# Short store runs beside long load runs, and Exp ahead of Ln, at the end of a streaming log-sum-exp scan

## Chip, cores, metric

One core of one Trainium2 chip. The metric is the device time of one execution in microseconds (us). A ratio is the mean time of one kernel's runs over that of the other's runs of the same rounds, so it is not quite the ratio of the medians quoted beside it. The span of a profile is about 1.7 us shorter than the time of the same run.

## The reference

For x of shape 8 x 4096 x 2048 (float32), a running log-sum-exp along the second axis:

```python
out[:, 0, :] = x[:, 0, :]
for t in range(1, S):
    mx = np.maximum(out[:, t-1, :], x[:, t, :])
    out[:, t, :] = mx + np.log(np.exp(out[:, t-1, :] - mx) + np.exp(x[:, t, :] - mx))
```

The kernel computes it as Ln of the prefix sum of Exp, 268 MB in and 268 MB out.

## The kernel before

A tile is 128 partitions x 4 rows x 2048 columns, 4 MiB; there are 64, numbered 0 to 63. A partition's four rows are neighbours in memory, so a whole tile moves as 128 runs of 32 KiB (a run is one contiguous piece, one record of data in the trace), 8 for each of 16 DMA engines (1213 ns a run in the trace). Four input buffers `ti`, two output buffers `to`. SP issues the loads, ACT issues the stores; the profile has one queue for each (q1 for loads, q10 for stores). A turn, below, is one record that an engine takes from one of its two queues. The semaphore write with which a DMA ends on an engine is a record of its own, of 4 bytes and 9 ns. The profile does not number the engines; what the text says of one engine was put together from the records, each of which begins where another ends, to 3 or 4 ns. While both queues hold work, the engines alternate between them: from 50 to 1110 us of this trace 15674 of 15767 records have one successor that no other record could have, and it is of the other queue every time, after the 1746 semaphore writes among them too.

```python
def exp(n, h, ...):                 # h: half of the columns
    if h == 0: take(act, loaded[n % NI], 16)
    act.activation(t[..half(h)], t[..half(h)], ACT.Exp).then_inc(exps[h], 1)

def ln(n, h, turn, in_place=False):
    if h == 0 and not in_place:
        take(act, stored[n % NO], 16)          # store of tile n-2 has left the buffer
    act.activation((ti if in_place else to)..., ti..., ACT.Ln)._wait_ge(carried[h], turn + 1)
# main loop, tiles 0..59
exp(n, 0); exp(n, 1); ln(n - 1, 0, ..); ln(n - 1, 1, ..)
event(act, [(logs, 2 * n)], [(freed, "sem-add-imm", 1)])   # lets SP load tile n + 3
act.dma_start(out=o_v[..][0], in_=to[(n - 1) % NO][:])
# ... the end, tiles 60..63, Ln in place in ti (no buffer wait):
for n in range(first + 1, NT):
    up = n - 1
    if n < NT - 1:
        exp(n, 0); exp(n, 1); ln(up, 0, .., True); ln(up, 1, .., True); store(up)
    else:                                      # n == 63
        ln(up, 0, .., True); exp(n, 0); ln(up, 1, .., True); store(up); exp(n, 1)
for h in range(2):
    ln(NT - 1, h, .., True); store(NT - 1, h)   # last store in two halves, runs of 4 KiB
```

DVE does six adds of row to row per tile, and two "joins" that add the carries from PE to all rows.

The softmax here doesn't subtract the row's maximum and nothing guards it: scores larger than these inputs give would overflow.

## Time and profile before

| | before |
|---|---|
| time, median of 4 runs | 1253.85 us (1253.28 to 1257.28) |
| span of the profile | 1252.5 us |
| DVE busy, ACT busy | 82%, 73% |
| moved | 537 MB at 429 GB/s |

The prediction below shows the slices and ACT's end. Here is the timeline of DVE from tile 60 on (start, duration, operation; in brackets how long DVE had stood idle before it, and for whom):

```profile
1161.74 7.40 DVE L248 TENSOR_TENSOR ti<-ti 128x1024 f32<-128x1024 f32 x6 [3.26 <-ACT ti L133]
1169.36 8.75 DVE L257 TENSOR_TENSOR ti<-ti,ps 128x4096 f32<-128x4096 f32 x2 [0.22 <-PE ps L224]
1181.60 7.40 DVE L248 TENSOR_TENSOR ti<-ti 128x1024 f32<-128x1024 f32 x6 [3.49 <-ACT ti L133]
...
1219.52 3.74 DVE L248 TENSOR_TENSOR ti<-ti 128x1024 f32<-128x1024 f32 x3 [5.58 <-ACT ti L133]
1227.06 3.75 DVE L248 TENSOR_TENSOR ti<-ti 128x1024 f32<-128x1024 f32 x3 [3.79 <-ACT ti L133]
```

A tile costs DVE 7.40 + 8.75 us. The waits in brackets are for Exp: DVE is not the bound of the kernel, but in the last tiles, where no more work overlaps, its holes count. The last two lines are tile 63: its first Exp half came behind an Ln half of tile 62, its second behind the other half.

### The profile page before, as it was taken

The numbers are of one execution on the slowest core, as the hardware profiler recorded it, in microseconds if no ns is written. First come the engines' busy times: TensorE is split into PE (matmuls) and PEld (weight loads), VectorE is DVE, ScalarE is ACT, GpSimd is POOL, SyncE is SP. The second block draws the span as 40 slices with busy tenths as digits, with TensorE's granted clock in tenths as the row PEclk, the third lists the DMA queues.
The fourth block names the chain that finished last, engine by engine and source line by source line (L and its number), as shares of the span: only waits on it lengthen the run. The fifth ranks groups of instructions, "written<-read, shape, count | busy, mean of one in ns | idle before, by whom it ended". The sixth has DMA issues, their size and how long they took to land. (4 is left out here: it accounts for less than half of the span.)

```text
span 1252.5 us, 3677 instructions
## 1 busy us (share of the span) xinstructions
PE 649.2 (52%) x960; PEld 214.1 (17%) x960; DVE 1023.0 (82%) x512; ACT 913.2 (73%) x258; POOL 1.1 (0%) x8
## 2 busy tenths in 40 slices
PE   2565356563664545546455553465545655346552
PEld 0121112121121211112112111121111111111110
DVE  5999788797887977878778788787887878878784
ACT  5886776777767668677686776867768668676884
POOL 0000000000000000000000000000000000000000
PEclk9988687876868868788687787877867777688785
DMA  9999999999999999999999999999999999999997
GB/s 402 419 435 434 429 433 431 433 433 435 435 434 430 432 431 433 434 434 435 434 430 432 431 433 434 434 435 434 429 434 430 433 434 435 434 434 429 435 430 303
DMA packets 19490, 536.90 MB, mean 429 GB/s; under 512 B 2080, under 2 KB 2080, under 8 KB 3104
## 3 DMA queue, kind: packets, MB, share of 16 engines
q1 hardware_dynamic: 9360, 268.44, 49.8%
q10 hardware_dynamic: 10128, 268.44, 49.7%
q8 instruction: 1, 0.02, 0.0%
q14 instruction: 1, 0.01, 0.0%
HBM read 268.44 MB, written 268.44 MB: 429 GB/s over the span
## 5 line engine op out<-in xcount | busy, mean ns | idle before, releaser
L248 DVE TENSOR_TENSOR ti<-ti 128x1024 f32<-128x1024 f32 x384 | 464.7, 1224 | 206.9 <-ACT ti L133 198.2
L140 ACT ACTIVATE to<-ti 128x4096 f32<-128x4096 f32 x120 | 427.6, 3609 | 248.4 <-ACTq L62 244.7
L257 DVE TENSOR_TENSOR ti<-ti,ps 128x4096 f32<-128x4096 f32 x128 | 560.0, 4417 | 9.5 <-PE ps L224 9.0
L224 PE MATMUL ps<-ti,before 128*128 128x512 f32 x512 | 381.2, 896 | 351.5 <-DVE ti L248 351.0
L133 ACT ACTIVATE ti<-ti 128x4096 f32<-128x4096 f32 (+1 forms) x128 | 452.6, 3582 | 59.9 <-ACTq L62 59.4
L213 PE MATMUL ps<-ti,last 128*128 128x512 f32 x448 | 268.2, 729 | 233.9 <-DVE ti L257 233.9
L224 PEld LDWEIGHTS ps<-ti,before 128*128 128x128 f32 x512 | 128.9, 279 | 617.9 <-DVE ti L248 510.8
L213 PEld LDWEIGHTS ps<-ti,last 128*128 128x128 f32 x448 | 85.3, 211 | 401.0 <-DVE ti L257 335.5
L140 ACT ACTIVATE ti<-ti 128x4096 f32<-128x4096 f32 x8 | 28.7, 3606 | 14.6 <-PEq L62 8.9
L153 ACT ACTIVATE ti<-ti 128x4096 f32<-128x4096 f32 x1 | 3.6, 3616 | 6.3 <-ACTq L62 6.3
L34 ACT ACT_TABLE_LOAD x1 | 1.3, 1283 | 0.8 <-PEq L286 0.8
L106 POOL TENSOR_SCALAR_AFFINE_SELECT last<-last 128x128 f32<-128x128 f32 x1 | 0.3, 295 | 0.0
L101 POOL TENSOR_SCALAR_AFFINE_SELECT before<-before 128x128 f32<-128x128 f32 x1 | 0.3, 294 | 0.1
L97 POOL MEMSET before<- 128x128 f32 x1 | 0.2, 205 | 0.5 <-SPq L80 0.5
L98 POOL MEMSET last<- 128x128 f32 x1 | 0.2, 205 | 0.0
L286 POOL MEMSET const-bfloat16-1.0<- 128x1 bf16 x1 | 0.1, 102 | 0.0
L286 POOL MEMSET const-uint8-127<- 128x1 uint8 x1 | 0.1, 102 | 0.0
L286 POOL MEMSET const-float32-0.0<- 128x1 f32 x1 | 0.1, 99 | 0.3 <-issue 0.3
L286 POOL MEMSET const-float32-1.0<- 128x1 f32 x1 | 0.1, 99 | 0.0
## 6 DMA issues: line engine op xcount, KB each, us to landing
ti<-in_x_dram SPq DMA_DIRECT2D x63, 4096.0 KB, 33.9
out_dram<-to ACTq DMA_DIRECT2D x60, 4096.0 KB, 31.4
out_dram<-ti ACTq DMA_DIRECT2D x3, 4096.0 KB, 22.4
ti<-in_x_dram SPq DMA_DIRECT2D x2, 2048.0 KB, 9.5
out_dram<-ti ACTq DMA_DIRECT2D x2, 2048.0 KB, 7.4
```

The costliest lines, as they stand in the source:

```text
L34: nc.scalar.preload_act_table_set("natural_log_exp_and_others")
L97: g.memset(before[:], 1.0).then_inc(ones, 1)
L101: g.affine_select(out=before[:], in_=before[:], compare_op=mybir.AluOpType.is_ge, fill=0.0, base=-1, pattern=[[1, P]], channel_multiplier= ...
L106: g.affine_select(out=last[:], in_=last[:], compare_op=mybir.AluOpType.is_ge, fill=0.0, base=-(P - 1), pattern=[[0, P]], channel_multiplier=1,
L133: act.activation(t[:, rows, half(h)], t[:, rows, half(h)], ACT.Exp).then_inc(exps[h], 1)
L140: act.activation((ti[n % NI] if in_place else to[n % NO])[:, :, half(h)], ti[n % NI][:, :, half(h)], ACT.Ln,)._wait_ge(carried[h], turn + ...
L153: act.activation(ti[0][:, 0:2, :], ti[0][:, 0:2, :], ACT.Exp)
L213: m = pe.matmul(ps[(k + 1) % 2][:, sl], last[:], ti[k % NI][:, R - 1, sl], start=True, stop=False, skip_group_check=True,)
L224: m = pe.matmul(ps[k % 2][:, sl], before[:], ti[k % NI][:, R - 1, sl], start=k == 0, stop=True, skip_group_check=True,)
L248: a = dve.tensor_add(t[:, r, half(h)], t[:, r - 1, half(h)], t[:, r, half(h)])
L257: dve.tensor_add(t[:, :, half(h)], t[:, :, half(h)], ps[n % 2][:, half(h)].unsqueeze(1).to_broadcast([P, R, HALF]),)._wait_ge(ahead[h], n ...
L286: nc = _bacc.Bacc("TRN2", target_bir_lowering=False, num_devices=1)
```

## The change

The intent: while the last loads are in flight, cut the stores into short runs, so that the DMA engines, which in the records alternate between the queues (all of those 15674 pairs), give the loads the larger part; and at the end do Exp of the next tile before Ln of the tile above, so that DVE gets its work early. The main loop ends four tiles sooner. The stores of tiles 56 to 59 become four DMAs of one row each (8 KiB runs); the last store becomes one again. The diff, cut to its core:

```diff
+                for n in range(first + 1, first + NI + 1):      # tiles 56..59
+                    up = n - 1
+                    exp(n, 0)
+                    exp(n, 1)
+                    ln(up, 0, up - first, stores_of=R if up >= first + NO else 1)
+                    ln(up, 1, up - first)
+                    event(act, [(logs, 2 * (n - first))], [(freed, "sem-add-imm", 1)])
+                    for r in range(R):
+                        act.dma_start(
+                            out=o_v[up][:, r, :], in_=to[up % NO][:, r, :]
+                        ).then_inc(stored[up % NO], 16)
... (cut)
-                    else:
-                        ln(up, 0, up - first, True)
-                        exp(n, 0)
-                        ln(up, 1, up - first, True)
-                        finals += store(up)
-                        exp(n, 1)
-                for h in range(2):
-                    ln(NT - 1, h, NT - 1 - first, True)
-                    finals += store(NT - 1, h)
+                    if n < NT:
+                        exp(n, 0)
+                        exp(n, 1)
+                    ln(up, 0, up - first, in_place=True)
+                    ln(up, 1, up - first, in_place=True)
+                    act.wait_ge(logs, 2 * (n - first))
+                    act.dma_start(out=o_v[up], in_=ti[up % NI][:]).then_inc(final, 16)
```

More of the change, by code (lines that the diff above doesn't have):

```diff
@@ L135, in exp, with ln @@
                     ).then_inc(exps[h], 1)
-                def ln(n, h, turn, in_place=False):
+                def ln(n, h, turn, in_place=False, stores_of=1):
                     if h == 0 and not in_place:
-                        take(act, stored[n % NO], 16)
+                        take(act, stored[n % NO], 16 * stores_of)
                     act.activation(
@@ L155, in _ @@
                 exp(0, 1, slice(2, R))
-                turns = (NT - 2) // NI
+                turns = (NT - 2) // NI - 1
                 with act.Fori(0, turns) as j:
@@ L171, in _ @@
                 first = turns * NI
-                finals = 0
-                def store(n, h=None):
-                    cols = slice(0, D) if h is None else half(h)
-                    act.wait_ge(logs, 2 * (n - first) + (2 if h is None else h + 1))
-                    act.dma_start(
-                        out=o_v[n][:, :, cols], in_=ti[n % NI][:, :, cols]
-                    ).then_inc(final, 16)
-                    return 1
-                for n in range(first + 1, NT):
-                    up = n - 1
-                    if n < NT - 1:
+                for n in range(first + 1, first + NI + 1):
+                    up = n - 1
+                    exp(n, 0)
[7 more added lines that the diff above has]
+                        ).then_inc(stored[up % NO], 16)
@@ L185, in _ @@
+                settle(NI)
+                first += NI
+                for n in range(first + 1, NT + 1):
+                    up = n - 1
+                    if n < NT:
                         exp(n, 0)
                         exp(n, 1)
-                        ln(up, 0, up - first, True)
-                        ln(up, 1, up - first, True)
-                        finals += store(up)
-                    else:
-                        ln(up, 0, up - first, True)
-                        exp(n, 0)
-                        ln(up, 1, up - first, True)
-                        finals += store(up)
-                        exp(n, 1)
@@ L196, in _ @@
-                for h in range(2):
-                    ln(NT - 1, h, NT - 1 - first, True)
-                    finals += store(NT - 1, h)
+                    ln(up, 0, up - first, in_place=True)
+                    ln(up, 1, up - first, in_place=True)
+                    act.wait_ge(logs, 2 * (n - first))
+                    act.dma_start(out=o_v[up], in_=ti[up % NI][:]).then_inc(final, 16)
                 settle(NT - first)
                 for n in range(NO):
-                    take(act, stored[n], 16)
@@ L202, in _ @@
-                take(act, final, 16 * finals)
+                    take(act, stored[n], 16 * R)
+                take(act, final, 16 * (NT - first))
             @block.tensor
```

## The prediction

Its sum: 1243.7 + 1.3 + 9.7 + 1.8 = 1256.5 us of span, and 1257.2 us of time.

> **What bounds the kernel now.** The kernel handles 64 tiles of 4 MiB (4 MiB in, 4 MiB out): Exp on ACT, prefix sums on DVE with carries from PE, Ln on ACT, store. I number tiles 0 to 63 by their stores in the timeline. I read the slices first, for what is full all the way:
>
> ```profile
> DMA  9999999999999999999999999999999999999997
> GB/s 402 419 435 434 429 433 431 433 433 435 435 434 430 432 431 433 434 434 435 434 430 432 431 433 434 434 435 434 429 434 430 433 434 435 434 434 429 435 430 303
> ```
>
> The DMA engines are full from start to end; only the last slice (31 us) has a hole. So a change at the end can win only what lies in that hole. The windows put it between 1234 and 1240:
>
> ```profile
> core 0: us, PE busy (x) PEld busy (x) DVE busy (x) ACT busy (x) POOL busy (x), PEclk, DMA share, GB/s
> 1234.50:1238.40 3.90, 0.14 (x1) 0.00 (x0) 3.90 (x2) 3.14 (x1) 0.00 (x0) 0.94 0.06 25
> 1240.30:1250.40 10.10, 0.00 (x0) 0.00 (x0) 0.00 (x0) 2.91 (x1) 0.00 (x0) 0.50 1.02 406
> ```
>
> A share of 0.06 is one engine of 16. In the packet records one engine falls behind all the others through the run, to some 5 us; it finishes the store of tile 62 at 1238.5, the others at 1233.7, and the first packet of the last store moves at 1240.2. So that engine has only 1.7 us of hole, and this, not 6.5 us, is the most that filling the hole can win.
>
> Next the timeline of ACT, for what decides when tiles come:
>
> ```profile
> start us, us, engine line op out<-in xcount [idle before <-releaser]
> 1150.24 7.12 ACT L140 ACTIVATE to<-ti 128x4096 f32<-128x4096 f32 x2 [4.49 <-ACTq L62]
> 1157.61 0.35 ACTq L165 DMA_DIRECT2D out_dram<-to  x1
> 1158.09 7.12 ACT L133 ACTIVATE ti<-ti 128x4096 f32<-128x4096 f32 x2 [0.72 <-ACTq L62]
> ...
> 1223.41 3.62 ACT L133 ACTIVATE ti<-ti 128x4096 f32<-128x4096 f32 x1 [0.42 <-ACT ti L140]
> 1235.26 3.62 ACT L140 ACTIVATE ti<-ti 128x4096 f32<-128x4096 f32 x1 [8.23 <-PEq L62]
> 1238.91 0.62 ACTq L177 DMA_DIRECT2D out_dram<-ti  x1
> 1239.59 3.62 ACT L140 ACTIVATE ti<-ti 128x4096 f32<-128x4096 f32 x1 [0.71 <-PEq L62]
> 1243.24 0.54 ACTq L177 DMA_DIRECT2D out_dram<-ti  x1
> ```
>
> The first line is Ln of tile 58. It waited 4.49 us in its queue for the store of tile 56 to leave the same output buffer: that store's completion, by the latest engine, came at 1150.13. The loads are ahead: that of tile 60 was in at 1152.6, its Exp (third line) began at 1158.09. The completion of stores, not of loads, paces the kernel. The chain at the end is
>
> ```profile
> 1235.06 4.42 DVE ti L257
> ...
> 1239.59 3.62 ACT ti L140
> ```
>
> the last DVE add, the last half Ln. Only half a tile remains to be stored after that, for the other half was issued at 1238.91.
>
> [...] loads (q1) and stores (q10) alternate after every single 32 KiB run (1213 ns each), and even the 4-byte semaphore write takes a whole turn (load, semaphore write, load). So turns are by descriptor whatever its size, and I predict with that. [...] Ln of tile 58 started 0.11 us after the latest engine's completion. [...] one lags here, but the records do not number it[...].
>
> **The change part by part.**
> (1) Stores of tiles 56 to 59 become four of 1 MiB in 8 KiB runs. An engine then has 32 runs per tile instead of 8. Single runs took 1213 ns at 32 KiB, 611 at 16 KiB, 162 at 4 KiB; between these I estimate 308 ns for 8 KiB. Per pair of turns a load moves 32 KiB and a store 8 KiB, so the loads get 4/5. On the slowest engine the store of tile 56 is at the head of its queue from 1130.2. In before, about 8 load runs pass beside its 8, and it ends at 1149.7. Now one run of load 59 and all 16 of loads 60 and 61 pass before its 32 turns are over: 17 x 1.213 + 32 x 0.308 = 30.5 us, so 1160.7, 11 us later. Load 62 cannot use the advantage, because it is issued only after Ln of tile 58, which waits for this very store. I add 0.47 + 0.11 us to Ln of tile 58 (1161.3), 7.12 for it, 0.25, and four issues instead of one (about 0.42 each): Exp of tile 60 starts at E = 1170.5 instead of 1158.1. The fast engines, 5 us ahead, even run dry for about 4 us, as the store of tile 57 ends at 1166 and new work comes at 1170.
> (2) Exp first at the end. From E on, DVE is what counts: 7.40 (six adds) + 0.22 + 8.75 (two joins) = 16.37 us a tile, four tiles, starting 3.65 us after E. Is ACT always in time? Exp of tile 61 comes after Exp 60 (7.12), Ln 59 (7.2), four issues and the settling (2.4): E + 16.7, its first half at E + 20.3, when DVE wants it at E + 20.0: 0.3 us lost. Then Ln 60, store, Exp 62 from E + 31.5, first half E + 35.1, wanted E + 36.7; Exp 63 from E + 46.3, first half E + 49.9, wanted E + 53.1. Both in time, and loads 62 and 63 are in by about 1185 and 1200 (issue, 1.3 us, eight pairs of turns). So with Exp first DVE never starves: its chain ends at E + 3.65 + 4 x 16.37 + 0.3 = E + 69.5 = 1240.0. In before it ended at 1239.48 after 77.7 us from the first add of tile 60 (1161.74) with 12.3 us of holes. The new order takes out these holes, the late Exp 60 costs 12.4: they cancel.
> (3) The last store in one piece. The last Ln ends 3.7 us after DVE, 1243.7, and then 4 MiB remain, not 2. From before, 1.28 us from issue to first packet and 1.8 us from last packet to the end of the span; 8 runs of 1213 ns are 9.7 us. Sum 1243.7 + 1.3 + 9.7 + 1.8 = 1256.5, against 1252.5: 4.0 us, of which 0.5 is the chain and 3.5 the missing split (9.7 us against the 5.2 us of a half in 4 KiB runs, less 1.0 us for which the second half waited behind the first). Earlier stores do not reach so far: store 62 issues at E + 60.8 = 1231 and ends near 1243. On the time of before: 1253.8 + 4.0 = 1257.8; a little less for the rivals: 1257.2.
>
> **Rivals.**
> (A) Turns by bytes, or by more than one run: then loads and stores keep half each, store 56 ends on time, E is about 1159. Exp 63 starts when its load lands (1211) instead of 1215.9 and 1223.4, DVE ends near 1231, the last store is issued at 1235, and behind store 62 it leaves the slow engine at about 1248.5: span 1250, time about 1251.5. For it speaks only that the trace has no two queues with data runs of unlike size; the turn taken by 4 bytes speaks against it.
> (B) 8 KiB runs cost more beside loads than I took. Every 0.03 us a run is 1 us on store 56, and goes into E and the end one for one: 1258 to 1260.
> (C) Eight stores in the queue at once block ACT at issue. ACT has about 10 us to spare before Ln 58, so mostly nothing, but 1 to 2 us more are possible if it hits the issue before Exp 60.
> (D) Everything is hidden by DMA anyway: the byte count is unchanged, and if the DMA engines stayed full the span would be 1250.8 at the least (1252.5 - 1.7). Against it: the last store waits for its Ln.
>
> **Range and chances.** All paths lie between 1251 and 1261. My own is 1257 to 1258 with about 1.5 us for run length and issue, (A) has perhaps one chance in seven; the runs of before themselves spread from 1253.3 to 1257.3. Time 1257.2, range 1252.3 to 1261. Two per cent is 25 us, more than the tail can move; 0.985 for the same, the rest split towards slower.
>
> **What would show it.** Right: a wait of about 15 us, not 4.5, ahead of Ln of tile 58; its start near 1161; Exp of tile 60 near 1170; loads 60 and 61 in about 8 and 15 us earlier than before (1152.6 and 1172.0); DVE nearly without holes over the last four tiles; a last store of 4096 KB issued near 1243.7 that takes some 11 us. Wrong: Ln 58 at 1150 (turns not by run), DVE waiting for Exp 62 or 63, or a last store that queues behind store 62 beyond 1245.

## The result, and the profile after

1257.93 us (median of 4 runs, 1257.56 to 1258.40) against 1253.85: ratio 1.0027, 95% interval 1.0009 to 1.0045. Slower by a quarter of a per cent; predicted were 1257.2 us. The span is 1255.9 us.

The slices of the changed kernel:

```profile
DMA  9999999999999999999999999999999999999997
GB/s 401 415 434 434 434 434 432 433 431 433 434 431 432 433 433 434 434 434 430 434 434 434 434 434 433 433 430 433 434 431 432 434 433 433 434 433 425 386 428 318
```

The hole in the last slice is still there, and a new one stands in the third slice from the end, 386 GB/s. ACT's timeline shows where it comes from:

```profile
1160.57 7.12 ACT L140 ACTIVATE to<-ti 128x4096 f32<-128x4096 f32 x2 [12.67 <-ACTq L62]
1167.80 2.00 ACTq L180 DMA_DIRECT2D out_dram<-to  x4
1169.94 7.12 ACT L133 ACTIVATE ti<-ti 128x4096 f32<-128x4096 f32 x2 [2.24 <-ACTq L62]
1176.97 7.11 ACT L140 ACTIVATE to<-ti 128x4096 f32<-128x4096 f32 x2
1184.18 2.90 ACTq L180 DMA_DIRECT2D out_dram<-to  x4
...
1239.65 3.62 ACT L140 ACTIVATE ti<-ti 128x4096 f32<-128x4096 f32 x1 [0.71 <-PEq L62]
1243.30 0.34 ACTq L195 DMA_DIRECT2D out_dram<-ti  x1
```

The first line is Ln of tile 58. Its wait for the store of tile 56 has grown from 4.49 to 12.67 us, it starts at 1160.57 instead of 1150.24, and Exp of tile 60 at 1169.94 instead of 1158.09. Until Ln of tile 58 is done no load can be issued (load 62 goes out at 1167.91), and the stores that are in the queue run out: in the packet records 15 of the 16 DMA engines stand still for 1.4 to 3.2 us around 1167. And yet the last Ln ends at the same time as in before (last issue 1243.30, in before 1243.24). DVE shows why:

```profile
1173.59 7.40 DVE L245 TENSOR_TENSOR ti<-ti 128x1024 f32<-128x1024 f32 x6 [12.79 <-ACT ti L133]
1181.20 8.75 DVE L254 TENSOR_TENSOR ti<-ti,ps 128x4096 f32<-128x4096 f32 x2 [0.22 <-PE ps L221]
1191.12 7.40 DVE L245 TENSOR_TENSOR ti<-ti 128x1024 f32<-128x1024 f32 x6 [1.17 <-ACT ti L133]
...
1223.47 7.39 DVE L245 TENSOR_TENSOR ti<-ti 128x1024 f32<-128x1024 f32 x6
1230.78 8.74 DVE L254 TENSOR_TENSOR ti<-ti,ps 128x4096 f32<-128x4096 f32 x2
```

One long hole ahead of tile 60, then next to none: 12 us lost before, 12 us of holes gone after. What stays is the last store, issued at the same moment but of 4 MiB instead of 2: its last packet ended at 1254.05, in before at 1250.67. That is 3.4 us, the whole loss of the profile. The records also show the DMA engines idle twice at the end: from 1228.6 nearly all of them stand still for about 3 us, and from 1241.5 all 16 for about 2.6 us, waiting for the next store to be issued. The end is set by the chain of DVE and Ln, not by the bytes.

### The profile page after: what moved, and what is told of

Same layout as the page of the kernel before. It is cut to its first block, busy times and chain, and to the rows that moved or that the text cites. A ratio compares the mean times of both kernels' runs of the same rounds, so it can differ in the third digit from the quotient of the medians.

```text
span 1255.9 us, 3677 instructions
## 1 busy us (share of the span) xinstructions
PE 640.1 (51%) x960; PEld 212.2 (17%) x960; DVE 1023.1 (81%) x512; ACT 913.1 (73%) x258; POOL 1.1 (0%) x8
## 5 line engine op out<-in xcount | busy, mean ns | idle before, releaser
L221 PE MATMUL ps<-ti,before 128*128 128x512 f32 x512 | 376.4, 887 | 349.4 <-DVE ti L245 348.7
L210 PE MATMUL ps<-ti,last 128*128 128x512 f32 x448 | 263.8, 718 | 243.4 <-DVE ti L254 243.4
```

The costliest lines, as they stand in the source:

```text
L210: m = pe.matmul(ps[(k + 1) % 2][:, sl], last[:], ti[k % NI][:, R - 1, sl], start=True, stop=False, skip_group_check=True,)
L221: m = pe.matmul(ps[k % 2][:, sl], before[:], ti[k % NI][:, R - 1, sl], start=k == 0, stop=True, skip_group_check=True,)
```

## The experiments

On each of three chips, the kernel before ran in the same rounds. The diffs are cut to their core: where an edit changes how many stores a later wait counts, that line is left out, and `...` stands for the rest of a line. The diff of rows_only is told in words.

**1. rows_only**: the row stores, with the order and the split of before at the end.

```diff
 (the changed kernel's loop for tiles 56..59, then)
-                    ln(up, 0, ...); ln(up, 1, ...)          # Exp first, one last store
+                    the end of the kernel before, from "finals = 0"
```

> The row stores alone, with the order and the split of before at the end. My theory: Exp of tile 60 is 12 us late as in the changed kernel, and the old order adds its holes after it, so they do not cancel: Ln 62 first half 1222 to 1225.5, Exp 63 first half to 1229, second half to 1236.6, DVE ends at 1249, last half store issued at 1252.9, end of data 1260.2, span 1262, time about 1263.3, ratio 1.0077. Rival (row stores alone are nearly free because the end is slack, or because loads come earlier): within 2 us of before, ratio below 1.0016.

Measured: 1263.66 us (1262.75 to 1273.59) against 1255.39, ratio 1.0071 (1.0038 to 1.0105); span 1261.0. From ACT's timeline:

```profile
1160.07 7.12 ACT L140 ACTIVATE to<-ti 128x4096 f32<-128x4096 f32 x2 [12.52 <-ACTq L62]
...
1251.82 0.54 ACTq L192 DMA_DIRECT2D out_dram<-ti  x1
```

Ln of tile 58 is late as in the changed kernel, and the old order adds its holes after it, as DVE's timeline shows for tiles 61 and 63 (brackets):

```profile
1191.18 7.40 DVE L263 TENSOR_TENSOR ti<-ti 128x1024 f32<-128x1024 f32 x6 [1.65 <-ACT ti L133]
...
1228.11 3.74 DVE L263 TENSOR_TENSOR ti<-ti 128x1024 f32<-128x1024 f32 x3 [4.90 <-ACT ti L133]
1235.65 3.74 DVE L263 TENSOR_TENSOR ti<-ti 128x1024 f32<-128x1024 f32 x3 [3.79 <-ACT ti L133]
```

The last issue comes at 1251.82 instead of 1243.24. The row stores alone cost 8.5 us (1261.0 - 1252.5, spans of profiles; 8.3 by the medians). The near draw of the whole change hides two large parts of opposite sign.

**2. exp_first_whole**: the changed kernel without the row stores.

```diff
-                    for r in range(R):
-                        act.dma_start(out=o_v[up][:, r, :], in_=to[up % NO][:, r, :]) ...
+                    act.dma_start(out=o_v[up], in_=to[up % NO][:]) ...
```

> The changed kernel without the row stores: Exp first, one last store of 4 MiB, all runs of 32 KiB. My theory: Ln 58 starts at 1150.2 and Exp 60 at 1158.1 as before, Exp 63 starts when its load lands (1211), DVE ends at 1231, the last store is issued at 1235 and queues behind store 62; the latest DMA engine never idles and ends at 1248.2, span 1250.0, time 1251.3, ratio 0.998: faster than both by 2.5 and 6.6 us. Rival (the row stores are needed so that the last loads come in time): DVE starves for loads, time not under that of before.

Measured: 1251.05 us (1250.94 to 1251.93), ratio 0.9957 (0.9933 to 0.9981). The ratio flatters it, because on that chip the runs of before spread from 1253.48 to 1261.13; against their best it is 2.4 us. From its ACT timeline:

```profile
1209.07 7.12 ACT L133 ACTIVATE ti<-ti 128x4096 f32<-128x4096 f32 x2 [1.92 <-ACTq L62]
...
1234.10 0.34 ACTq L194 DMA_DIRECT2D out_dram<-ti  x1
```

Exp of tile 63 waited 1.92 us for its load, the only load wait of the end; the last store, now in one piece, was issued 9.1 us earlier than the last half in before. The packet records of the latest DMA engine show no gap over 0.4 us any more; it ends at 1247.42 (predicted 1248.2). The other 15 have ended by 1245.2. So this version ends when its latest engine has moved its bytes. The loads did not need help.

**3. late_rows_whole**: row stores only for tiles 58 and 59, on which no later Ln waits.

```diff
-                    for r in range(R):
+                    for r in (range(R) if up >= first + NO else [slice(0, R)]):
```

> Row stores only for tiles 58 and 59, on whose completion no later Ln waits; tiles 56 and 57 whole, the rest as in the changed kernel. My theory: nothing waits for the slowed stores, Ln 58 at 1150.2, Exp 60 near 1159.2, the loads 62 and 63 land earlier than in before (load 63 near 1196 instead of 1211), DVE ends near 1231, and the latest DMA engine sets the end: time 1251.0 to 1252.0, within 0.7 us of the version without rows, ratio 0.998. Rival (runs of 8 KiB beside loads cost DMA time in themselves): 2 us or more over the version without rows.

Measured: 1251.46 us (1251.16 to 1251.83), ratio 0.9977 (0.9964 to 0.9990). From ACT's timeline:

```profile
1151.03 7.12 ACT L140 ACTIVATE to<-ti 128x4096 f32<-128x4096 f32 x2 [4.57 <-ACTq L62]
...
1209.25 7.12 ACT L133 ACTIVATE ti<-ti 128x4096 f32<-128x4096 f32 x2 [0.50 <-ACTq L62]
```

Ln of tile 58 starts at 1151.03, and Exp of tile 63 no longer waits for its load, which landed at 1194.39, but starts straight after an issue. The time is within 0.4 us of experiment 2, which ran on another chip, and under that of experiment 9 on the same chip. Runs of 8 KiB beside loads cost no time that shows; what costs is that an Ln waits for them.

**4. two_16k**: tiles 56 to 59 in two DMAs each, runs of 16 KiB.

```diff
-                    for r in range(R):
-                        ... o_v[up][:, r, :] ... to[up % NO][:, r, :]
+                    for r in range(2):
+                        ... o_v[up][:, 2 * r:2 * r + 2, :] ... to[up % NO][:, 2 * r:2 * r + 2, :]
```

> The changed kernel, tiles 56 to 59 stored in two DMAs each of two rows, runs of 16 KiB. My theory: what delays store 56 is the loads that are in the queue (one run and two whole loads), not the ratio 4 to 1; 16 turns of 0.611 still let about 16 load runs of 1.213 pass: store 56 ends 29.2 us after 1130.2, Ln 58 starts near 1160, two issues less bring Exp 60 to about 1168.3, time about 1256, ratio 1.0017 (a little less if the order of semaphore turns favours it). Rival (the delay grows with the number of runs, so half of it with 16 KiB): Ln 58 near 1155.5, Exp 60 near 1164, time about 1253, ratio below 1.0.

Measured: 1254.67 us (1254.15 to 1258.59), ratio 1.0010 (0.9995 to 1.0026).

```profile
1159.65 7.12 ACT L140 ACTIVATE to<-ti 128x4096 f32<-128x4096 f32 x2 [13.79 <-ACTq L62]
1166.88 0.85 ACTq L180 DMA_DIRECT2D out_dram<-to  x2
1167.87 7.12 ACT L133 ACTIVATE ti<-ti 128x4096 f32<-128x4096 f32 x2 [1.09 <-ACTq L62]
...
1182.11 1.28 ACTq L180 DMA_DIRECT2D out_dram<-to  x2
```

Ln of tile 58 is as late as with 8 KiB (1159.65), as my theory had it: the loads that are in the queue pass it either way. The rival's half delay (1155.5) is refuted; experiment 6 counts the turns. The time came out 1.3 us under what I expected: I had counted two issues fewer once. They lie twice on the path, ahead of Exp 60 and ahead of Exp 61 (0.85 and 1.28 us instead of 2.00 and 2.90), which with the 0.9 us of the earlier Ln makes 3.7 us; last issue 1239.89 instead of 1243.30. The 0.9 us is no effect of the store: this profile is ahead by 1.0 us already at Ln of tile 57 (1130.52 against 1131.52).

**5. four_32k**: four DMAs each, but by 32 partitions, so that runs stay 32 KiB.

```diff
+                        ps_ = slice(32 * r, 32 * r + 32)
-                            out=o_v[up][:, r, :], in_=to[up % NO][:, r, :]
+                            out=o_v[up][ps_], in_=to[up % NO][ps_]
```

> The changed kernel, tiles 56 to 59 stored in four DMAs each, but cut by partitions (32 partitions each), so that every run stays 32 KiB. My theory (a turn is one run whatever its size, so only the run length shifts the shares): store 56 ends on time, Ln 58 starts at 1150 to 1151, Exp 60 near 1159.5, last store near 1236, time about 1251.5 to 1252.5, ratio 0.999. Rival (four DMAs instead of one are what delays the store): Ln 58 near 1160, time 1257.9, ratio 1.003.

Measured: 1265.49 us (1263.33 to 1271.23), ratio 1.0092 (1.0073 to 1.0112). Slower than everything, and not for the reason tested. ACT's timeline:

```profile
1156.13 7.12 ACT L140 ACTIVATE to<-ti 128x4096 f32<-128x4096 f32 x2 [3.19 <-ACTq L62]
1163.37 8.08 ACTq L181 DMA_DIRECT2D out_dram<-to  x4
```

Four issues took 8 us, and in the records many 32 KiB runs of stores took about 2.55 us, single ones up to 3.3 us, between 1162 and 1171. (The profile fell on the slowest of the six executions.) The DMA view of 1163.5 to 1171 agrees: some 50 runs of stores at 2.06 us on average (85.7% of 16 engines for 7.5 us), in before 49 at 1.22 us. Why stores of 32 neighbouring partitions were slow is not shown. So the experiment mixes a slow transfer into the question and decides nothing about it.

**6. four_strided**: the same with every fourth partition, `ps_ = slice(r, P, R)`.

> As four_32k, but each of the four DMAs takes every fourth partition, so that each DMA is spread over all partitions as a whole tile is. In four_32k a run of 32 KiB took up to 2.5 us when its store was alone and an issue took 2 us, which mixed a slow transfer into the test. My theory (only the run length shifts the shares; a contiguous quarter of the partitions is what was slow): runs take 1.21 us again, store 56 ends on time, Ln 58 starts at 1150 to 1151, Exp 60 near 1160, time 1251.0 to 1253. Rival (it is four DMAs instead of one that delay the store): Ln 58 near 1160, time near 1257.

Measured: 1256.62 us (1256.28 to 1262.85), ratio 1.0031 (1.0015 to 1.0047).

```profile
1153.86 7.12 ACT L140 ACTIVATE to<-ti 128x4096 f32<-128x4096 f32 x2 [5.96 <-ACTq L62]
1161.10 2.43 ACTq L181 DMA_DIRECT2D out_dram<-to  x4
1163.67 7.12 ACT L133 ACTIVATE ti<-ti 128x4096 f32<-128x4096 f32 x2 [2.68 <-ACTq L62]
1175.81 7.12 ACT L140 ACTIVATE to<-ti 128x4096 f32<-128x4096 f32 x2 [5.02 <-ACTq L62]
```

My expectation of 1251 to 1253 was wrong, and the sharper part of it, that only the run length matters, falls. While the runs were back at 1.21 us, Ln of tile 58 came 3.6 us late (1153.86 against 1150.24). That is the size of three turns: a DMA ends on every engine with a 4-byte semaphore write, which in the records takes a turn of its own (in before a record of the other queue follows each of the 1746 above), and four DMAs have three more of them than one; 3 x 1.21 = 3.6. Counted on one engine from the end of store 55 to the end of store 56, runs and semaphore writes together:

| | turns of the store | turns of loads beside them | load runs among these | Ln 57 to Ln 58 |
|---|---|---|---|---|
| before | 9 | 9 | 8 | 19.46 us |
| four_strided | 12 | 12 | 11 | 22.88 us |
| two_16k | 18 | 18 | 16 | 29.13 us |
| changed kernel | 36 | 18 (13 of 16 engines) | 16 | 29.05 us |

The load runs more than in before, times 1.21 us, are 3.6, 9.7 and 9.7 us; from Ln 57 to Ln 58 it takes 3.4, 9.7 and 9.6 us longer. (Counted so, an offset of up to 1 us between two profiles drops out.) Load and store take turn for turn, until the loads in the queue are used up: with 8 KiB runs there would be turns for twice as many, but there are no more. That is why 16 and 8 KiB give the same delay. Then Ln of tile 59 waited as well (5.02 us in the last line, for the store of tile 57, which now ran beside load 62). Exp of tile 61 so began at 1186.29, only 1.2 us ahead of the changed kernel, and the last store was issued 1.3 us ahead (1242.02): that made the time. The rival's mechanism (all of the delay from the number of DMAs, Ln 58 at 1160) is wrong too, it is 3.4 of some 10 us; its time, near 1257, came out by another way.

**7. last_whole and last_whole_again**: the kernel before, with only its last store in one piece.

```diff
                 for h in range(2):
                     ln(NT - 1, h, NT - 1 - first, True)
-                    finals += store(NT - 1, h)
+                finals += store(NT - 1)
```

> The kernel before with its last store in one piece, nothing else. My theory: last Ln ends at the same 1243.2, then 1.28 + 9.7 us of data instead of 7.4: 3.5 us later, time 1257.4, ratio 1.0028. Rival (the last store is bound by the DMA backlog of the late engine, not by its issue): at most 1 us later, ratio below 1.0008.

Measured: 1257.99 us (1256.43 to 1262.48), ratio 1.0010 (0.9985 to 1.0036): inconclusive, the runs of before spread too far on that chip. On another chip:

> The kernel before with its last store in one piece, again, because the first time the runs of before on that chip spread over 7 us and the profile fell on a run with its loads late by 5 us. My theory: 3.3 us over before (from issue to last packet 10.75 us in the first profile, 7.43 in before), ratio 1.0026. Rival: below 1.0008.

Measured: 1257.68 us (1256.94 to 1257.79) against 1253.84 (1253.20 to 1255.53), ratio 1.0028 (1.0015 to 1.0041). In the profile the last Ln ended as ever and the store was issued at 1243.19; its last packet ended at 1253.94. The one piece costs 3.3 us in the records (10.75 us from issue to last packet, 7.43 in before), as predicted; by the medians it is 3.8 us.

**8. split_last and split_last_again**: the changed kernel with its last store in halves again.

```diff
+                    if n == NT:
+                        for h in range(2):
+                            ln(up, h, up - first, in_place=True)
+                            act.wait_ge(logs, 2 * (up - first) + h + 1)
+                            act.dma_start(out=o_v[up][:, :, half(h)], in_=ti[up % NI][:, :, half(h)]) ...
+                        continue
```

> The changed kernel with its last store in two halves again. My theory (missing split): the chain up to the last Ln stays (last issue near 1243.3 in the span), but the first half is issued near 1239, runs behind store 62 from 1241.5 to 1246.7, the second half to 1251.9; so 2.1 us less than the changed kernel, time 1255.8, ratio to before 1.0016. Rival (8 KiB runs cost bandwidth, and that is the loss): the split gives nothing, 1257.9, ratio 1.003.

Measured: 1256.14 us (1255.91 to 1262.56), ratio 1.0005 (0.9976 to 1.0033), again with the spread of that chip.

> The changed kernel with its last store in halves, again, now on the same chip as the changed kernel itself. My theory: 2.1 us under the changed kernel (the first half has to wait for store 62 until 1241.5), ratio to before 1.0016. Rival (the split is worth its full 3.5 us): ratio 1.000.

> The changed kernel unedited, as the yardstick for the other three on this chip: 1257.9, ratio 1.003.

Measured on the one chip: split 1256.41 us (1255.72 to 1273.49, ratio 1.0045, 1.0004 to 1.0086, driven by the one run of 1273), the changed kernel 1257.81 us (1257.54 to 1261.92), ratio 1.0036 (1.0023 to 1.0048). By the medians the split gives back 1.4 us, by the spans of the profiles 1.8 (1254.4 against 1256.2), not the 3.3 that it is worth in the kernel before. In its profile the first half was issued at 1239.80, but its packets ended only at 1247.5: it stood behind the store of tile 62, whose last packet ended at 1242.4; the second half followed at once and ended at 1252.65. The direction is clear and near the 2.1 us expected, but the interval of the ratio alone would not carry it.

**9. exp_first_split**: experiment 2 with the last store in halves.

> Exp first, no row stores, last store in two halves. My theory: once Exp is first, the end is set by the bytes of the latest DMA engine and not by the last Ln, so the split gains nothing and its 4 KiB runs (162 ns each, 10.4 us for a tile instead of 9.7) cost 0.7 us: time 1252.0 against 1251.3 with one store, ratio 0.9986. Rival (the split is worth its 3.5 us whatever the order): time 1248.

Measured: 1251.93 us (1251.34 to 1252.10), ratio 0.9980 (0.9968 to 0.9993). On the chip of experiment 3, 0.5 us above that version's 1251.46 (which differs by its late row stores too); 0.9 us above experiment 2, on another chip. The latest DMA engine again shows no gap over 0.3 us in its records and ends at 1247.86. With Exp first, the split gains nothing, because the end is a matter of bytes. The rival's 1248 is refuted.

## Why the prediction was right, point by point

- **The share of the queues.** Ln of tile 58 was predicted for 1161.3, it came at 1160.57; an 8 KiB run for 308 ns, it took 309; loads 60 and 61 for 8 and 15 us earlier, they landed 9.2 and 16.5 earlier than in the profile of before (1143.35 and 1155.51), 6.9 and 14.2 earlier than in that of last_whole_again, which has the same loop; loads 62 and 63 for about 1185 and 1200, they landed at 1184.7 and 1200.9. One size was off: I had 17 load runs beside the store, the records have 16 on most engines, 1.2 us less. That the start fits within 0.7 us is in part luck, as the changed kernel's profile runs 0.74 us late already at Ln of tile 57 (1131.52 against 1130.78). The wait ahead of Ln 58 was 12.67 us and not 15, because Exp of tile 59 before it came 2.15 us later as well (1140.78 against 1138.63), behind four issues of 1.89 us. Experiment 1 shows what the delay costs, experiments 4 and 6 the turns behind it, of semaphore writes too. In the changed kernel the semaphore writes make no difference, for the queued loads are all past before the store ends (load 61 landed at 1155.51, the store at 1160.46). Rival (A), turns by bytes, is refuted.
- **Exp of tile 60 late.** Predicted E = 1170.5, measured 1169.94, from four issues of 2.00 us together where I had 4 x 0.42 (an estimate; a single issue took 0.35 us in before). The fast engines ran dry for about 2.5 us; I had said 4.
- **Exp first.** Predicted that it takes 12.3 us of holes out and so cancels the delay, with DVE's end at 1240.0: measured 1239.52, in before 1239.46. Two terms were off and offset each other. DVE lost 1.17 us before tile 61, not 0.3, because the four issues ahead of Exp 61 took 2.90 us; and a tile takes DVE 16.15 us (7.40 + 8.75), not 16.37, where it does not have to wait 0.22 us for PE. And I gave the new order too much of the credit: in rows_only, in the old order, the hole ahead of tile 61 is already 1.65 us instead of 3.49, for Ln of tile 59 no longer waits for its buffer when Exp of tile 60 is late. Experiments 1 and 8 show what the order itself is worth with the row stores in place: the last issue moves from 1251.82 to 1243.87, 8.0 us, and the span from 1261.0 to 1254.8 or 1254.4, 6.2 to 6.6 us (7.5 by the medians of the same rounds).
- **The last store in one piece.** Predicted 3.5 us, measured alone 3.3 (experiment 7). What I did not say ahead of the result: taking it back in the changed kernel returns only some 1.5 us, as the store of tile 62 is then in the way.
- **The sum.** 1256.5 of span predicted, 1255.9 measured. With the row stores gone the same kernel does 1251.05: leaving them out is enough to turn the loss into a gain. The last store in one piece costs something only as long as the end waits for the last Ln (experiments 7 and 8), and nothing once it does not (experiment 9).
- **Rival (D)**, that DMA hides everything, holds only for the versions without the wait (experiments 2, 3 and 9), which all end within 1 us of each other. (B) did not show: the 8 KiB run cost what was estimated. Of (C) there was a little: the wait ahead of Ln 58 swallowed the longer issue after Ln 57, but the issues ahead of Exp 60 took 2.00 us where 1.7 had been counted, and those ahead of Exp 61, with the settling (resetting semaphores), 3.4 us where 2.4 had been counted; that stores already in the queue made the issues longer is not shown. What made one DMA engine late stays open (the store of tile 62 in before ended there at 1238.5, on 13 of the others by 1233.8 and on the other two by 1235.0; in the changed kernel at 1230.1 against 1228.8).

## What to carry to other kernels

Where DMA engines alternate between a load queue and a store queue one record at a time, as they did here (9 turns to 9 in before, 18 to 18 in two_16k), run length is a priority: short runs yield (here the store of one tile let 16 load runs pass instead of 8; with 8 KiB runs it ended some 10 us later, and two loads landed 7 to 9 and 14 to 16.5 us earlier). More DMAs also took ACT longer to issue: one 4 MiB store 0.35 us, four of 1 MiB in rows 1.9 to 3.8 us, four by 32 neighbouring partitions up to 8.1 us. Before you slow a stream in this way, look up who waits for it; a store that frees a buffer is on the path of the next load. And when a change hardly moves the time, test its parts alone: here one part cost 8.5 us, another gave 6, and leaving out the first made the fastest version.
